# A Conformer block on eight cores: GLU blocks transposed in order and read by the conv matmuls with a step, W_v in halves, the conv finish spread over the output tiles

## The chip, the cores and the metric

The kernel runs on all 8 cores of one Trainium2 chip (trn2), two dies of four cores. Each core computes one of the 8 batch items on its own; nothing is exchanged. The metric is the device time of the slowest core in microseconds (us), median of several executions. Executions fall in a fast and a slow state: in the slow one the cores of a die show a lower granted TensorE clock (0.94 to 0.95 on cores 0 to 3 and 0.99 on cores 4 to 7 in the changed kernel's slow run of 2925 us). Only fast runs are compared here. Engines are PE (TensorE matmul), PEld (its weight loads), DVE (VectorE), ACT (ScalarE), POOL (GpSimd) and the DMA queues issued from SP and POOL.

## The reference, cut to what matters

```python
h = rms_norm(x)                              # x: (8, 2048, 2048) float32
u = h @ w_in                                 # conv value | conv gate | q | k | v, 1024 columns each
g = c_val * sigmoid(c_gate)                  # GLU
y = causal depthwise conv of g, width 31     # per channel, over the sequence
y = silu(layer_norm(y + b_dw))               # LayerNorm over the 1024 channels
a = chunked attention(q, k, v)               # 8 heads, band of 9 chunks of 64
x = x + concat(rms_norm(y), rms_norm(a)) @ w_out
x = x + relu(rms_norm(x) @ w1)**2 @ w2       # the FFN
```

## The kernel before

A small scheduler in the kernel's own Python code records operations with their dependencies, simulates them with rough durations, and so fixes the order of each engine's instructions. On the chip each engine is given its list in that order. `SLACK` is an extra delay that this simulation adds before a matmul may use what another engine produced; it changes only the order.

The stages, in order of time: V projection for 16 tiles of 128 positions; attention with the query and key projections; gates and depthwise conv for 8 blocks of 128 channels; the "finish" of the conv branch (normalisation and swish, by quarters of the sequence) between W_out tiles; FFN.

The depthwise conv runs on PE. A gated block `G` (128 channels x 512 positions) is transposed in 32x32 blocks into `Gt`. Then for each of 32 places `i` in a block of 32 two matmuls with small block-diagonal weights are made. Their moving operand is a row of `Gt` over 64 blocks (32 in the last two channel blocks):

```python
    Gt = [sb(f"Gt{i}", [32, 66], BF16, ...) for i in range(2)]     # place i, then block
    # conv_gate(cc, qd):
        stt(G[:, :], th[:, :], 1.0, ps(1), ALU.add, ALU.mult)      # the GLU
        o_ = bass.AP(gt, 1 + 16 * qd, [[32 * 66, 128], [1, 16], [66, 32]])
        P.vtr(o_, G[:, :].rearrange("p (b i) -> p b i", i=32), slow=3.6)
    # conv_dw(cc, q0, nq, bank):   n = 16 * nq
        for ih in range(2):
            ...                                                    # POOL builds the weights `pad`
            for i in range(16):
                mm(o_, pad[:, i, 0, :], gt[:, 16 * ih + i, c0:c0 + n], True, False)
                mm(o_, pad[:, i, 1, :], gt[:, 16 * ih + i, c0 - 1:c0 - 1 + n], False, True)
```

So the transpose writes 2-byte elements 132 bytes apart, and the matmul reads contiguous columns.

The V projection takes W_v in quarters of 256 columns, each loaded in one piece; quarters 2 to 4 wait for certain x tiles:

```python
        for hf in range(4):
            for k in range(16):
                mm(ps(hf, 0, 256), hT[:, qd, k, ti * 128:(ti + 1) * 128], wv[:, hf, k, :], k == 0, k == 15)
            act(V[:, t, 2 * hf:2 * hf + 2, 0:128], ps(hf, 0, 256)..., AF.Identity)
    for j in (1, 2, 3):
        ld[j].deps.add(xo_[2 * j - 1].i)          # quarter j waits for x tile 2j-1
```

## Time and profile before

| | before |
|---|---|
| time, 3 fast runs | 2785.1 us median (2784.4 to 2786.53) |
| PE busy | 2707 of 2782 us (97%) |
| DVE, ACT busy | 34%, 30% |
| start of the last V matmul (median of cores) | 181.6 us |

The first fence holds lines of the profile's page for the kernel before: busy time by engine, and the chain of work that ended last as shares of the span.

```profile
PE 2707.2 (97%) x14445; PEld 1327.1 (48%) x14704; DVE 932.3 (34%) x1482; ACT 830.9 (30%) x1601; POOL 228.1 (8%) x365
...
PE 94%; DMA 2%; issue 2%; DVE 1%; ACT 1%; ACTq 0%; DVEq 0%; SPq 0%; POOLq 0%
```

The chain says that nearly all of the time is PE's (94%). So in this kernel time taken from another engine should be worth something only where PE waits for it, and time added on PE should be added to the whole.

The next view is busy time by stretches, on the slowest core (core 0). The columns are the stretch, its length, then busy us (and instructions) of each engine, the granted clock (1.00 is full), the DMA share and GB/s.

```profile
0.00:20.00 20.00, 9.71 (x27) 4.46 (x28) 5.35 (x12) 6.68 (x9) 2.11 (x8) 1.00 0.87 214
20.00:40.00 20.00, 9.60 (x79) 7.13 (x77) 10.24 (x10) 11.30 (x19) 0.72 (x2) 0.83 1.01 232
40.00:60.00 20.00, 8.95 (x70) 6.93 (x70) 7.05 (x8) 8.01 (x12) 0.53 (x1) 0.66 1.00 290
60.00:80.00 20.00, 15.11 (x120) 12.01 (x118) 5.24 (x6) 9.48 (x18) 0.00 (x0) 0.83 0.46 162
...
720.00:740.00 20.00, 17.28 (x111) 7.98 (x110) 19.89 (x24) 10.92 (x15) 7.83 (x8) 1.00 1.00 207
```

PE stands half idle at the start, with the DMA engines full. At 720 us it waits for 2.7 of 20 us, and DVE has no free time there (19.89 of 20).

Two lines of the timeline show the conv matmuls (start, length, engine, line, operation, output <- inputs, count): a run of 32 with 64 columns takes 1.13 us, one with 32 columns 0.96 us.

```profile
518.91 1.13 PE L159 MATMUL ps<-Gt_112,pad 128*128 128x64 bf16 x32
...
702.82 0.96 PE L159 MATMUL ps<-Gt_112,pad 128*128 128x32 bf16 x32
```

And the groups of instructions by form (busy us, mean ns of one, idle time before) for the DVE transposes: the strided write takes 2.46 us, a transpose of the same 128x512 out of PSUM 0.73.

```profile
L206 DVE STREAM_TRANSPOSE Gt_112<-G 128x512 bf16<-128x512 bf16 x16 | 39.3, 2458 | 1.5
L206 DVE STREAM_TRANSPOSE Gt_113<-G 128x512 bf16<-128x512 bf16 x16 | 39.3, 2456 | 1.5
L206 DVE STREAM_TRANSPOSE y<-ps 128x512 f32<-128x512 f32 x32 | 23.3, 727 | 8.8 <-PE ps L159 7.9
```

### The profile page before, as it was taken

The page shows a single profiled execution, that of the slowest core. Times are in us where ns is not written, and L with a number is a line of the kernel's source. Part 1 is how long each engine was busy: PE and PEld are TensorE (multiplying, and loading weights), DVE is VectorE, ACT ScalarE, POOL GpSimd, SP SyncE. Part 2 cuts the span into 40 slices and gives each one's busy share as a digit, 9 for nine tenths or more (in the row PEclk, how much of TensorE's full clock was granted, in tenths as well). Part 3 has the DMA queues.
Part 4 walks back from the last instruction along what each step waited for, and adds up shares of the span by engine and source line. Part 5 has one row for each costly group of instructions (what it writes and reads, how often), then busy time and mean ns, then how long its engine had stood idle before and what let it go on. Part 6 is the DMA issues. An engine that isn't in the chain of part 4 may idle for free.

```text
span 2782.1 us, 38484 instructions; the slowest of 8 cores (2778.2 to 2782.1 us)
## 1 busy us (share of the span) xinstructions
PE 2707.2 (97%) x14445; PEld 1327.1 (48%) x14704; DVE 932.3 (34%) x1482; ACT 830.9 (30%) x1601; POOL 228.1 (8%) x365
## 2 busy tenths in 40 slices
PE   4999999999989999999999999999999999999999
PEld 3875555444444544444444444444444444444444
DVE  3236665655787522022131130220311302202113
ACT  4428887311376431211202102112022021120120
POOL 0000000422500000000000000000000000000000
PEclk8999999999999999999999999999999999999999
DMA  9411110324655478454444444579544444444424
GB/s 243 103 31 36 34 28 11 61 46 76 122 152 167 152 155 177 77 76 76 76 76 76 76 76 76 76 151 196 123 76 76 76 76 76 76 78 76 77 43 137
DMA packets 112455, 256.86 MB, mean 92 GB/s; under 512 B 5393, under 2 KB 83217, under 8 KB 94609
## 3 DMA queue, kind: packets, MB, share of 16 engines
q0 software_dynamic: 92112, 167.82, 37.9%
q1 hardware_dynamic: 20162, 86.56, 9.3%
q8 instruction: 122, 2.00, 0.3%
q14 instruction: 59, 0.48, 0.1%
HBM read 388.60 MB, written 33.55 MB: 152 GB/s over the span
## 4 chain that ended last, share of the span: by engine, by line
PE 94%; DMA 2%; issue 2%; DVE 1%; ACT 1%; ACTq 0%; DVEq 0%; SPq 0%; POOLq 0%
PE ps L159 93%; DMA xa_71<-x 1%; PE ps L163 1%; DMA acc<-out 1%; DMA wc_105<-wcg 0%; DVE y L198 0%; DVE y L192 0%; DVE hb_77 L198 0%; DVE Gt_113 L206 0%; ACT L178 0%; ACT hb_77 L178 0%; DVE hb_78 L198 0%; DVE y L206 0%; DVE yb L203 0%; DVE h2b L198 0%
## 5 line engine op out<-in xcount | busy, mean ns | idle before, releaser
L192 DVE TENSOR_TENSOR acc<-acc,ps 128x512 f32<-128x512 f32 x512 | 351.8, 688 | 1413.3 <-PE ps L159 1401.9
L159 PE MATMUL ps<-yb,fT 128*128 128x512 bf16 x2699 | 596.4, 379 | 4.0 <-DVE acc L192 1.1
L159 PEld LDWEIGHTS ps<-yb,fT 128*128 128x128 bf16 x2752 | 269.1, 98 | 326.3 <-issue 2.1
L178 ACT ACTIVATE rl_134<-ps 128x512 f32<-128x512 f32 x128 | 76.4, 597 | 1102.5 <-PE ps L159 1101.0
L159 PE MATMUL ps<-w2s_138,fT 128*128 128x512 bf16 x1317 | 292.4, 379 | 1.4
L159 PE MATMUL ps<-hTb,yb 128*128 128x512 bf16 x1024 | 242.2, 379 | 0.0
L159 PE MATMUL ps<-yb 128*128 128x512 bf16 x992 | 237.6, 379 | 1.7
L159 PEld LDWEIGHTS ps<-w2s_138,fT 128*128 128x128 bf16 x1344 | 131.5, 98 | 158.6
L225 POOL DMA_DIRECT2D yb<-w x75 | 66.6, 888 | 1173.8 <-PE ps L159 1105.6
L159 PEld LDWEIGHTS ps<-yb 128*128 128x128 bf16 x1024 | 100.2, 98 | 120.8
L159 PEld LDWEIGHTS ps<-hTb,yb 128*128 128x128 bf16 x1024 | 100.2, 98 | 120.3
L178 ACT ACTIVATE rl_135<-ps 128x512 f32<-128x512 f32 x128 | 76.4, 597 | 271.1 <-PE ps L159 271.1
L159 PE MATMUL ps<-wv,hT 128*128 128x256 bf16 x1024 | 120.6, 281 | 5.4 <-DMA wv<-wv 4.0
L159 PE MATMUL ps<-hTb,w1s_136 128*128 128x512 bf16 x512 | 121.0, 379 | 0.0
L159 PE MATMUL ps<-hTb,w1s_137 128*128 128x512 bf16 x512 | 121.0, 379 | 0.0
L159 PE MATMUL ps<-wo,yT 128*128 128x512 bf16 x497 | 117.1, 383 | 3.9 <-ACT yT L178 2.2
L159 PE MATMUL ps<-yb,w1s_136 128*128 128x512 bf16 x480 | 119.3, 379 | 1.7
L159 PE MATMUL ps<-yb,w1s_137 128*128 128x512 bf16 x496 | 117.5, 379 | 0.8
L159 PE MATMUL ps<-hT,wc_105 128*128 128x512 bf16 x498 | 115.0, 381 | 3.4 <-DMA wc_105<-wcg 2.5
L159 PE MATMUL ps<-hT,wc_104 128*128 128x512 bf16 x496 | 117.4, 379 | 0.9
L159 PE MATMUL ps<-wo,yb 128*128 128x512 bf16 x496 | 113.4, 379 | 0.8
L159 PEld LDWEIGHTS ps<-wv,hT 128*128 128x128 bf16 x1024 | 102.6, 101 | 20.6 <-issue 6.3
(300 smaller groups left out, 2741.1 us busy)
## 6 DMA issues: line engine op xcount, KB each, us to landing
yb<-w POOLq DMA_DIRECT2D x75, 1024.0 KB, 10.2
w2s_138<-w POOLq DMA_DIRECT2D x21, 1024.0 KB, 9.5
w1s_136<-w POOLq DMA_DIRECT2D x16, 1024.0 KB, 9.3
w1s_137<-w POOLq DMA_DIRECT2D x16, 1024.0 KB, 9.4
acc<-out SPq DMA_DIRECT2D x16, 1024.0 KB, 11.8
out<-acc SPq DMA_DIRECT2D x64, 256.0 KB, 7.5
wo<-wo POOLq DMA_DIRECT2D x8, 1024.0 KB, 13.4
xs_127<-x SPq DMA_DIRECT2D x6, 1024.0 KB, 6.4
```

The lines of the kernel that those rows point to most:

```text
L159: self.op("pe", lambda e: e.matmul(out, lhsT=lhsT, rhs=rhs, start=start, stop=stop, skip_group_check=skip), [lhsT, rhs], [out], f * max(n ...
L163: self.op("pe", lambda e: e.transpose(out, in_, ident), [in_, ident], [out], 64.0)
L178: self.op("act", lambda e: e.activation(out=out, in_=in_, func=func, scale=scale, bias=bias, **kw), r, w, d).func = func
L192: self._ew(eng, lambda e: e.tensor_tensor(out=out, in0=in0, in1=in1, op=op), [in0, in1], [out], fast)
L225: o = self.op(eng, lambda e: e.dma_start(out=out, in_=in_), r, w, 900.0 if eng == "pool" else 350.0, dma=True, key=key, nbytes=nb)
```

## The change

Its intent is to make the DVE transposes dense, to get the V projection going before all of W_v has landed, and to remove PE waits between the conv finish and the W_out tiles. The diff, cut to its core (an added `lazy` delay of zero is left out):

```diff
-SLACK = 400.0
+SLACK = 700.0
-    Gt = [sb(f"Gt{i}", [32, 66], BF16, ...)]
+    Gt = [sb(f"Gt{i}", [65, 32], BF16, ...)]
-        o_ = bass.AP(gt, 1 + 16 * qd, [[32 * 66, 128], [1, 16], [66, 32]])
-        P.vtr(o_, G[:, :].rearrange("p (b i) -> p b i", i=32), slow=3.6)
+        P.vtr(gt[:, 1 + 16 * qd:17 + 16 * qd, :], G[:, :].rearrange("p (b i) -> p b i", i=32))
-                mm(o_, pad[:, i, 0, :], gt[:, 16 * ih + i, c0:c0 + n], True, False)
-                mm(o_, pad[:, i, 1, :], gt[:, 16 * ih + i, c0 - 1:c0 - 1 + n], False, True)
+                mm(o_, pad[:, i, 0, :], gt[:, c0:c0 + n, 16 * ih + i], True, False)
+                mm(o_, pad[:, i, 1, :], gt[:, c0 - 1:c0 - 1 + n, 16 * ih + i], False, True)
...
-    wv_d = dr("wv", [4, 128, 16, 256])
+    wv_d = dr("wv", [2, 128, 16, 512])
+    # half 0 in 4 chunks of 4 k-blocks; x tile 1 waits for chunk 0, x tiles 2-4 for chunk 2
+        xo_[t].deps.add(ld[0 if t == 1 else 2].i)
+    # half 1 in 4 chunks, all waiting for x tile 3
+        o_.deps.add(xo_[3].i)
-        for hf in range(4):
+        for hf in range(2):
+            b = 2 * hf + t % 2
...
-    seq = [("c", 0), ("f", 1, 0, 4), ("a", 2), ("c", 1), ("f", 1, 4, 8), ("c", 2), ("s", 2), ("a", 3), ("c", 3), ("f", 2, 0, 3), ...
+    seq = [("c", 0), ("f", 1, 0, 2), ("a", 2), ("c", 1), ("f", 1, 2, 5), ("c", 2), ("f", 1, 5, 8), ("a", 3), ("c", 3), ("s", 2), ...
```

In `seq`, "a" and "c" are the attention and conv halves of a W_out tile, "s" the statistics of a quarter and ("f", q, i, j) the finish of its channel blocks i to j-1.

The moving operand of a conv matmul now has its columns 32 elements, 64 bytes, apart.

## The prediction

The forecast's sum came to -11 us, 2774 us in all. Its +11 us, for the conv matmuls that read with a step, was the author's estimate.

> **What bounds it now.** TensorE. The page's busy table gives PE 2707 of 2782 us, and the chain of waits is 94% PE. The timeline and the busy time by stretches show four stages:
> - 0-182 us, V projection. Its PE work is 16 tiles x (64 matmuls of 256 columns, 7.15 us, plus 16 transposes, about 0.9 us), about 129 us; so about 53 us are lost, all before 75 us. There the DMA engines are 87-101% busy to 60 us, an x tile (1 MB) takes about 4.4 us, PE waits for x and W_v, and the granted clock falls to 0.66-0.83.
> - 182-480, attention: PE 99% busy.
> - 480-980, conv, finish, W_out: PE 99% busy except 3 us at 660-672 (a gate weight load) and about 14 us at 720-820, where it waits for ScalarE and VectorE; VectorE is busy 19.9 of 20 us at 720-740.
> - 980-2776, FFN: matmuls back to back. Not touched.
>
> **What the change does.**
> 1. GLU transposes: 32 strided-output transposes of 2.456 us become dense. The PSUM-to-y transposes of the same 128x512 take 0.727 us, so I expect about 0.7 us: 56 us of VectorE saved. Nearly all is off the critical path; only those at 717-735 delay the first finish: 3 us gained.
> 2. Conv matmuls read their moving operand with a 64-byte step. Now 32 matmuls of 64 columns take 1.13 us, about 30 ns apart; 32 columns about 25 ns. [...]
> 3. W_v in 512-column halves: steady PE time is the same. Work on half 0 can start once 4 MB of W_v and x0 are in (about 25 us), and then each x tile (4.4 us of DMA) brings about 4.4 us of work while half 1 loads. PE should be mostly busy from about 28 us instead of 75 us, at 70-80% until half 1 has landed (about 65 us). V stage ends at about 168 instead of 182: 14 us gained (5 to 22).
> 4. Even finish: the waits at 784-803 (about 6 us on ScalarE results) mostly go: 5 us gained.
> 5. The larger scheduling slack only reorders; the added lazy term is zero. No effect that I can size.
>
> Sum: -14 + 11 - 3 - 5 = -11 us. **Predicted 2774 us**, 80% range 2758 to 2799. Faster by over 2%: 1%; within 2%: 98%; slower by over 2%: 1%.
>
> **What would show it.** First query/key projection matmul (182.4 us now) about 14 us earlier; PE busy at 20-60 us well above 18.5 of 40, its clock nearer 1. [...] GLU transposes about 0.7 us. VectorE busy down by about 55 us. PE idle at 720-820 about 6 us instead of 14. FFN unchanged at about 1797 us.
>
> **What would make it wrong.** The stride costing nothing (about 2763) or four times (about 2800). The start: PE runs a fixed order, so if half 1's matmuls stand ahead of ready half-0 work, chained loads leave it idle and the 14 us shrink or vanish.

## The result and the profile after

The three fast runs of the changed kernel take 2803.05 us in the median (2802.5 to 2805.2), those of the kernel before 2785.1. Each kernel had one slow run besides (2925 and 2999 us); with it the medians are 2804.12 and 2785.82. The ratio of fast runs is 1.0065, 95% interval 1.0043 to 1.0088. It is slower by about 18 us. Ratios here are the mean time of one kernel's fast runs over that of the other's of the same rounds, so they are not quite the ratio of the medians quoted.

Where the time went can be read from the first and last matmuls of each stage on each of the 8 cores (medians):

| stage | before | after | difference |
|---|---|---|---|
| start to the first gate matmul (V, attention) | 467.7 | 451.5 | -16.3 |
| first gate matmul to first W_out matmul | 262.9 | 302.3 | +39.4 |
| first W_out matmul to first W1 matmul | 302.2 | 297.1 | -5.1 |
| first W1 matmul to the end of the last matmul (FFN) | 1740.6 | 1740.6 | 0 |

Page line of the changed kernel: DVE is 53 us less busy, as forecast, and PE 40 us more.

```profile
PE 2747.7 (98%) x13917; PEld 1314.9 (47%) x14192; DVE 879.0 (31%) x1482; ACT 835.0 (30%) x1577; POOL 229.4 (8%) x369
```

The start, by stretches, again on the slowest core (core 4). PE is much busier at 40 to 60 us (17.00 instead of 8.95). At 20 to 40 us it still waits, and its clock is at half for nearly all of that time (0.51).

```profile
0.00:20.00 20.00, 12.02 (x32) 4.78 (x32) 5.35 (x12) 5.78 (x8) 3.36 (x10) 1.00 0.84 154
20.00:40.00 20.00, 7.92 (x30) 3.39 (x32) 3.17 (x3) 5.28 (x7) 2.12 (x4) 0.51 0.92 291
40.00:60.00 20.00, 17.00 (x108) 8.57 (x109) 14.11 (x13) 14.01 (x24) 0.00 (x0) 0.98 1.02 220
60.00:80.00 20.00, 16.12 (x87) 8.35 (x87) 3.82 (x4) 9.78 (x15) 0.00 (x0) 0.83 0.57 179
```

The transposes, by form: 0.71 us, as forecast.

```profile
L207 DVE STREAM_TRANSPOSE Gt_113<-G 128x512 bf16<-128x512 bf16 x16 | 11.4, 711 | 1.6
L207 DVE STREAM_TRANSPOSE Gt_112<-G 128x512 bf16<-128x512 bf16 x16 | 11.3, 709 | 1.3
```

The timeline of PE around the first conv block, and one run of 32 columns:

```profile
502.55 3.70 PE L160 MATMUL ps<-Gt_112,pad 128*128 128x64 bf16 x32
506.08 5.79 PE L160 MATMUL ps<-hT,wc_105 128*128 128x512 bf16 x25
511.70 3.70 PE L160 MATMUL ps<-Gt_112,pad 128*128 128x64 bf16 x32
515.23 1.00 PE L160 MATMUL ps<-hT,wc_105 128*128 128x512 bf16 x2
516.45 3.45 PE L160 MATMUL ps<-hT,wc_105 128*128 128x512 bf16 x10 [0.22 <-issue]
...
716.93 2.00 PE L160 MATMUL ps<-Gt_112,pad 128*128 128x32 bf16 x32
```

A run of 64 columns takes 3.70 us instead of 1.13, one of 32 columns 2.00 instead of 0.96; from start to start it is 110 and 57 ns per matmul instead of about 30 and 25. There are 12 of the first and 8 of the second: 12 x 2.57 + 8 x 1.04 = 39.1 us of added PE time, where I had forecast 11.

Look also at the gate matmuls (`hT,wc`) after each run. After the first, 25 of them take 5.79 us, the usual pitch of about 0.22 us. After the second, twelve stand in the 4.7 us from 515.23 to 519.90: about twice the usual spacing for most of that time (0.427 us from start to start; 0.216 is usual). There the clock was halved. The stretches show it; first the kernel before (500 to 700 us), then the changed one:

```profile
500.00:550.00 50.00, 48.86 (x335) 23.80 (x341) 27.55 (x32) 12.56 (x25) 26.59 (x26) 1.00 0.50 81
550.00:600.00 50.00, 49.71 (x277) 22.22 (x279) 28.89 (x26) 7.94 (x13) 11.94 (x13) 1.00 0.21 37
600.00:650.00 50.00, 49.47 (x326) 22.89 (x332) 31.92 (x29) 9.14 (x14) 19.25 (x19) 1.00 0.37 64
650.00:700.00 50.00, 47.02 (x287) 22.13 (x291) 25.31 (x21) 6.36 (x10) 13.99 (x16) 0.97 0.47 82
```

```profile
500.00:550.00 50.00, 49.51 (x276) 28.88 (x281) 16.75 (x24) 7.83 (x12) 20.43 (x21) 0.97 0.32 57
550.00:600.00 50.00, 49.56 (x246) 25.04 (x250) 14.77 (x21) 7.11 (x12) 9.88 (x10) 0.97 0.18 33
600.00:650.00 50.00, 49.73 (x265) 27.36 (x269) 13.20 (x18) 6.05 (x10) 13.12 (x14) 0.97 0.30 53
650.00:700.00 50.00, 49.08 (x253) 26.33 (x256) 19.40 (x26) 7.29 (x11) 16.54 (x17) 0.93 0.24 43
```

The clock column (third from the right) is where to look: 0.97 of 50 us is one stretch of 3.4 us at half clock, 0.93 is two. The clock record of the trace has 4 to 6 such stretches of 3.413 us between 495 and 700 us on each core of the changed kernel, 38 in all, and every one begins within 1 us of the end of a run of 32 strided matmuls. The kernel before has at most one, at 672 us, where PE waits for a gate weight load. And PE's busy column stays at 99%: on a busy engine this loss cannot be seen in the busy time.

### The profile page after: what moved, and what is told of

It reads as the page before. It is cut to its first block, busy times and chain, and to the rows that moved or that the text cites. A ratio compares the mean times of both kernels' runs of the same rounds, so it can differ in the third digit from the quotient of the medians.

```text
span 2803.6 us, 37361 instructions; the slowest of 8 cores (2795.3 to 2803.6 us)
## 1 busy us (share of the span) xinstructions
PE 2747.7 (98%) x13917; PEld 1314.9 (47%) x14192; DVE 879.0 (31%) x1482; ACT 835.0 (30%) x1577; POOL 229.4 (8%) x369
## 3 DMA queue, kind: packets, MB, share of 16 engines
q8 instruction: 117, 1.92, 0.3%
## 4 chain that ended last, share of the span: by engine, by line
PE 95%; DMA 2%; issue 1%; ACT 1%; DVE 1%; POOL 0%; SPq 0%; ACTq 0%; DVEq 0%; POOLq 0%
PE ps L160 94%; DMA wv<-wv 2%; PE ps L164 1%; DMA xa_74<-x 1%; ACT L179 0%; DVE y L199 0%; POOL pad L190 0%; POOL wv L226 0%; DVE y L193 0%; DVE yb L204 0%; ACT yb L179 0%; ACT h2b L179 0%; ACT y L179 0%; ACT yT L179 0%; ACT rs L179 0%
## 5 line engine op out<-in xcount | busy, mean ns | idle before, releaser
L160 PE MATMUL ps<-wv,hT 128*128 128x512 bf16 x497 | 117.6, 392 | 15.5 <-DMA wv<-wv 14.2
L160 PE MATMUL ps<-hT,wc_105 128*128 128x512 bf16 x499 | 120.6, 393 | 1.3 <-issue 0.7
L160 PE MATMUL ps<-hT,wc_104 128*128 128x512 bf16 x493 | 118.5, 383 | 0.8
L160 PE MATMUL ps<-hT,wqk_66 128*128 128x512 bf16 x374 | 95.9, 379 | 0.6
```

Source lines behind the costliest of these rows:

```text
L160: self.op("pe", lambda e: e.matmul(out, lhsT=lhsT, rhs=rhs, start=start, stop=stop, skip_group_check=skip), [lhsT, rhs], [out], f * max(n ...
```

## The experiments

Theory A: the strided moving operand makes the conv matmuls slower on PE itself, and the long runs of 32 slow matmuls also pull the clock down. Theory B: the new order (slack, finish) makes PE wait. "Before" in the tables is the kernel before, run in the same rounds on the same chip; times are medians of the fast runs. All kernels gave right results except sweep.

### Parts undone and parts alone

`dense` is the changed kernel with the old block layout:

```diff
-    Gt = [... [65, 32] ...]      # conv reads with a step of 32 elements
+    Gt = [... [32, 66] ...]      # conv reads contiguous columns, transposes write with a step
```

> The changed kernel with part 1 and 2 undone: the gated blocks are transposed with a step again, and the conv matmuls read 64 (or 32) contiguous columns; W_v halves, finish order and slack stay as changed. Theory A (the strided moving read costs PE time and drops the clock): runs of 32 conv matmuls of 64 columns back at 1.13 us (3.70 in the changed kernel), of 32 columns at 0.96 (2.00), no half-clock windows between 490 and 700 us, and the whole at about 2804 - 39 - 8 = 2757 us, so about 1% faster than the kernel before. Theory B (the loss comes from the new order: slack 700 and the finish spread): still about 2790 to 2804 us.

`before_stride` is the opposite, the kernel before with only the new block layout.

> The kernel before with part 1 and 2 of the change alone: dense block transposes, conv matmuls read with a 64-byte step. Theory A: about 2785 + 39 + 8 - 3 = 2829 us, conv runs of 3.70 us, several 3.4 us half-clock windows between 510 and 720 us. Theory B: 2785 us or less, since 56 us of VectorE work go.

`before_wv` is the kernel before with only the W_v part of the diff above.

> The kernel before with the W_v part alone (halves, chunks of 4 k-blocks, chained loads). From the stage ends of the changed kernel (first gate matmul 467 to 451 us, median of cores) theory A expects 16 us: 2769 us. If the start-up gain in the changed kernel came from the slack instead, about 2785.

| run | time | before, same rounds | ratio (95%) |
|---|---|---|---|
| dense | 2763.5 | 2784.1 | 0.992 (0.9892 to 0.9949) |
| before_stride | 2825.9 | 2784.1 | 1.0142 (1.0121 to 1.0163) |
| before_wv | 2762.7 | 2784.1 | 0.9917 (0.9897 to 0.9938) |

The layout costs 41.8 us alone and about 40 in the changed kernel (2803.1 - 2763.5). Theory B falls: without the layout the same order is faster than the kernel before. In dense the runs of 32 are back at 1.13 us, as this line of its timeline shows, and no core has a half-clock stretch between 455 and 700 us. Dense missed its expected 2757 by 6 us: that sum took 8 us for the clock and left out what the short transposes had gained.

```profile
503.32 1.13 PE L160 MATMUL ps<-Gt,pad 128*128 128x64 bf16 x32
```

W_v alone gives 21 us, more than the 16 expected. One thing did not fit: dense has W_v, the new finish order and the new slack, and is no faster than before_wv. That is taken up below.

### What the step costs: sweep, step4, step8

`sweep` reads the block buffer with a different step in each of the twelve runs of 64 columns:

```diff
+                sp = [1, 2, 3, 4, 5, 6, 8, 12, 16, 24, 31, 32][2 * cc + ih] if nq == 4 else 32
+                m_ = bass.AP(gt, i if nq == 4 else ..., [[2080, 128], [sp, n]])
```

The "line theory" of the next three records was a guess that no run had shown by then.

> Wrong result on purpose. The changed kernel; the twelve runs of 32 conv matmuls of 64 columns read the same block buffer with steps of 1, 2, 3, 4, 5, 6, 8, 12, 16, 24, 31 and 32 elements of 2 bytes, in that order of time. Line theory [...]: about 30 ns each up to step 4 (8 bytes), then a knee between 4 and 8, and from 8 (16 bytes) flat at about 110 ns whatever the step. Bank rival (large powers of two collide): 31 and 24 are much cheaper than 32 and 16. Plain-stride rival (any step but 1 is slow): step 2 is at 110 ns already.

`step4` and `step8` are right versions of the changed kernel, in which the buffer holds groups of g places (g = 4 and 8), so that a conv matmul reads with a step of g elements and the transpose writes runs of g elements:

```diff
-    Gt = [... [65, 32] ...]
+    Gt = [... [32 // g, 65, g] ...]
-        P.vtr(gt[:, 1 + 16 * qd:17 + 16 * qd, :], G[:, :].rearrange("p (b i) -> p b i", i=32))
+        o_ = bass.AP(gt, g * (1 + 16 * qd), [[2080, 128], [g, 16], [65 * g, 32 // g], [1, g]])
+        P.vtr(o_, G[:, :].rearrange("p (b a i) -> p b a i", a=32 // g, i=g))
```

> The changed kernel with the blocks stored in groups of four: the conv matmuls read with a step of 4 elements (8 bytes[...]), the block transposes write runs of 8 bytes. Line theory: conv runs of 32 take 1.13 us, no half-clock windows at 490 to 700, and the whole is as fast as the dense kernel (2764 us). Plain-stride rival: 3.7 us and about 2804 us. The block transposes should lie between 0.71 and 2.46 us; that changes the whole by under 3 us either way.

> The changed kernel with the blocks stored in groups of eight: a step of 16 bytes[...]. Line theory: as slow as the 64-byte step, 3.7 us for a run and 2804 us. Proportional rival (cost grows with the step): about a quarter of the loss, some 2775 us.

Sweep ran at 2793.7 us (one fast run; its time means nothing). Its timeline on core 0, the unbroken runs of 32 in order: steps 1, 2, 4, 5, 6, 8, 12, 16, 24, 31 and 32 (the run with step 3 was cut into pieces by other work; 29 of its 31 spacings can still be read):

```profile
492.80 1.12 PE L160 MATMUL ps<-Gt,pad 128*128 128x64 bf16 x32
499.36 1.17 PE L160 MATMUL ps<-Gt,pad 128*128 128x64 bf16 x32
...
518.81 2.11 PE L160 MATMUL ps<-Gt,pad 128*128 128x64 bf16 x32
545.76 2.55 PE L160 MATMUL ps<-Gt,pad 128*128 128x64 bf16 x32
553.76 2.98 PE L160 MATMUL ps<-Gt,pad 128*128 128x64 bf16 x32
581.58 3.87 PE L160 MATMUL ps<-Gt,pad 128*128 128x64 bf16 x32
590.90 3.87 PE L160 MATMUL ps<-Gt,pad 128*128 128x64 bf16 x32
619.61 3.93 PE L160 MATMUL ps<-Gt,pad 128*128 128x64 bf16 x32
630.67 3.80 PE L160 MATMUL ps<-Gt,pad 128*128 128x64 bf16 x32
663.09 3.71 PE L160 MATMUL ps<-Gt,pad 128*128 128x64 bf16 x32
671.60 3.69 PE L160 MATMUL ps<-Gt,pad 128*128 128x64 bf16 x32 [0.48 <-POOL pad L190]
```

From the starts of the matmuls in the trace, per matmul of 64 columns (a "line" is here 16 bytes of a partition, the step from which the spacing is flat; the lines touched are worked out from the step):

| step in elements (bytes) | ns from start to start | 16-byte lines touched | ns per line |
|---|---|---|---|
| 1 (2) | 29.8 | 8 | (does not show) |
| 2 (4) | 31.5 | 16 | (hardly shows) |
| 3 (6) | 46.0 | 24 | 1.92 |
| 4 (8) | 60.3 | 32 | 1.88 |
| 5 (10) | 74.1 | 40 | 1.85 |
| 6 (12) | 87.4 | 48 | 1.82 |
| 8 (16) | 115.3 | 64 | 1.80 |
| 12 to 16 | 115 to 117 | 64 | 1.80 to 1.83 |
| 24 to 32 | 110 to 113 | 64 | 1.71 to 1.77 |

The cost grows with the step up to 16 bytes and is flat after that. Steps of 31 and 24 are no cheaper than 32, so it is no collision of powers of two. Step 2 is nearly free, so it is not "any step but one" either. What fits all points is a charge of 1.7 to 1.9 ns for every 16 bytes touched, which does not show at steps 1 and 2 (29.8 and 31.5 ns), where such a line serves eight and four columns. This is an estimate from these spacings; no run looks inside the read. My line theory was right about the flat end from 16 bytes on, and wrong about the place of the knee: at step 3 the spacing is already 46 ns, and at step 4, where it still had about 30, it is 60.3, so the rate is half.

| run | time | before, same rounds |
|---|---|---|
| step4 | 2775.0 (ratio 0.9965, 0.9942 to 0.9988) | 2783.7 |
| step8 | 2808.5 (one fast run) | 2783.7 |

step4 missed its 2764 by 11 us; its runs of 64 columns take 2.10 us. The half rate costs 384 x 30 ns = 11.7 us, so the size fits, though not to the us: its three fast runs spread over 5.6 us. step8's runs take 3.88 us, and it is as slow as the 64-byte step.

### The clock by itself: interleave, interleave2

Here the strided matmuls stay, but later priorities set one or two dense gate matmuls between two of them:

```diff
+                if nq == 4:                  # interleave2: if nq == 4 and cc < 5:
+                    for e_ in (0, 1):
+                        P.ops[-1 - e_].prio = dw0 + 90 + 73 * ih + 1.5 * (2 * i + 1 - e_)
```

> The changed kernel, strided conv matmuls kept, but those of 64 columns are given later priorities, so that one to two dense gate matmuls stand between two of them. Theory A with the clock as a separate cost: each strided matmul still costs about 80 ns more than a dense one (30.8 us over 384), [...]the 4 to 6 half-clock windows at 490 to 700 us go and about 8 us come back: 2796 us. If the half-clock windows have another cause (waits, or fixed places in time), they stay and the time stays at 2804.

> As interleave, but the last of the six full conv blocks keeps its old priority, since in interleave a new wait of some 5 us stood at 697 to 707 us, where that block's late end held up the finish. In interleave the time from the 256th to the 640th gate matmul was 108.9 us without half-clock windows (changed kernel 112 with about two, dense 94.1). Clock as a separate cost: about 2804 - 6 = 2798 us. If the half-clock windows cost nothing, 2804 us.

interleave took 2805.4 us (three fast runs, ratio 1.0071, 1.0042 to 1.01), which missed the expected 2796: the late end of the last full block made a new wait just after 695 us. With that block left alone, interleave2 took 2797.9 (two fast runs, 2796.9 and 2798.9, where 2798 was expected). That is 5.2 us less than the changed kernel's 2803.05, or 3.7 less if each is taken against the kernel before in its own rounds: about 4 to 5 us. The stretches of interleave2 (its slowest core):

```profile
500.00:550.00 50.00, 50.00 (x282) 28.07 (x281) 12.76 (x19) 5.71 (x9) 13.95 (x15) 1.00 0.25 43
550.00:600.00 50.00, 50.00 (x266) 25.93 (x265) 19.64 (x28) 9.13 (x14) 15.00 (x15) 1.00 0.25 45
600.00:650.00 50.00, 50.00 (x273) 26.73 (x272) 13.80 (x19) 5.76 (x9) 13.95 (x14) 1.00 0.22 41
650.00:700.00 50.00, 48.87 (x259) 25.79 (x258) 18.63 (x25) 8.65 (x13) 16.10 (x17) 0.97 0.38 69
```

On all eight cores there is no half-clock stretch between 510 and 665 us, where the interleaved blocks run, and one at 669 to 685 us, at the one block left as it was. Cores 3 and 7 have one more, at 497 and 503 us. There the new priorities had left the very first run of 32 unbroken, and the stretch begins within 1 us of its end; on the other six cores the same run drew none. On the cores whose records are complete, the time over the first 640 gate matmuls is 161.1 us in dense, 179.3 in interleave2 (181 on cores 3 and 7), and 184 to 187 in the changed kernel. So some 18 us of that stage are the slow reads. The clock is 3.4 to 6.8 us more: by core, two to four stretches of 3.4 us at half speed. About 1 us of the difference is not accounted for. What is shown is that half-clock stretches began at the ends of unbroken runs of strided matmuls (all 38 in the changed kernel, after runs of 3.70 us), and that there were none where the runs were broken up. Why the clock falls there no run shows. In step4, whose runs take 2.1 us, no core has such a stretch between 505 and 700 us either; in sweep no core has one from 490 us on before the runs of 3.87 us begin, though those before it take up to 2.98.

### Finish order, slack and the W_v loads

`before_fin` is the kernel before with the new `seq` only; `before_slack` has `SLACK = 700.0` only; `wv_fin` is the W_v part and the new `seq` with the old slack (so dense with the slack back at 400).

> The kernel before with the new order of conv finish and W_out tiles alone (old slack, old transposes, old W_v). My prediction: 5 us faster, 2779. The dense kernel (W_v, order and slack: 2764) against before_wv (2763) says together nothing: then 2784, with the PE waits of 780 to 803 us gone but others come up at 720 to 760.

> The kernel before with the larger scheduling slack (700 instead of 400) alone. If the slack costs what the finish order gives: 2790 to 2795 us. If it only reorders, as predicted: 2784.

> The kernel before with the W_v part and the new finish order, but the old slack; dense (2764) with the slack back at 400. If the parts add up: 2763 - 9 = 2754 us, and the slack cost some 10 us in the changed kernel. If the finish order gains nothing once W_v is in halves: 2763.

| run | time | before, same rounds | difference |
|---|---|---|---|
| before_fin | 2774.7 | 2783.6 | -8.9 (ratio 0.9969, 0.9953 to 0.9984) |
| before_slack | 2791.8 | 2784.9 | +6.9 (ratio 1.0012, 0.998 to 1.0044) |
| wv_fin | 2754.2 | 2784.9 | -30.8 (ratio 0.9877, 0.9833 to 0.992) |

The ratios of the last two rows lean on one run of the kernel before that counts as fast at 2806.1 us; its six others lie at 2784.2 to 2785.3, and all five fast runs of before_slack at 2790.8 to 2792.7, so I take the 7 us as real although the interval holds 1. The stages agree: in before_slack the first gate matmul comes 3.5 us later than in the kernel before, and the stretch from the first W_out to the first W1 matmul is 4.2 us longer (306.4 against 302.2, medians of cores). In before_fin that stretch is 291.5. The lines for 780 to 800 us of the kernel before and of before_fin show the PE wait that went (15.20 and 20.00 us busy):

```profile
780.00:800.00 20.00, 15.20 (x113) 7.85 (x112) 12.53 (x21) 19.08 (x27) 0.00 (x0) 0.95 0.39 153
```

```profile
780.00:800.00 20.00, 20.00 (x128) 9.88 (x126) 17.14 (x27) 19.88 (x26) 0.00 (x0) 1.00 0.30 107
```

Finish order and slack cancel each other. For the finish order I had forecast 5 us and got 9; before_fin was expected at 2784, because I had read dense as "the finish order gives nothing", and that expectation missed. The larger slack, which I had put at zero, costs 7 us alone and 9 to 10 in the new order (dense 2763.5 against wv_fin 2754.2). The slack shifts waits to other places. Dense, then wv_fin, from 720 us (both on their slowest core):

```profile
720.00:740.00 20.00, 13.65 (x106) 6.28 (x104) 14.31 (x23) 12.43 (x20) 5.60 (x4) 0.74 0.47 100
...
780.00:800.00 20.00, 17.08 (x119) 8.82 (x117) 9.20 (x13) 18.00 (x23) 0.89 (x1) 0.97 0.59 171
```

```profile
720.00:740.00 20.00, 17.86 (x143) 8.47 (x141) 12.92 (x19) 10.34 (x16) 5.46 (x5) 0.74 0.37 77
...
780.00:800.00 20.00, 20.00 (x128) 9.95 (x127) 14.19 (x18) 14.92 (x22) 0.89 (x1) 1.00 0.69 186
```

PE is 4.2 and 2.9 us busier in these two stretches with the old slack. The larger slack also moves the last V matmul: 185 us in before_slack (median of cores), 181.6 in the kernel before.

`wv_nochain` is before_wv without the waits between x tiles and W_v chunks; `quarters_nochain` is the kernel before with its quarters, but without the waits that hold quarters 2 to 4 back:

> The kernel before with W_v in halves and the same eight chunk loads, but without the chain: x tiles 1 to 4 and the second half's chunks are issued at once. If the gain of 21 us comes from the order of the loads, x tiles and both halves now share the DMA engines from the start, the first half lands about twice as late and most of the gain is lost: 2775 to 2785. If it comes from the halves alone, 2763.

> The kernel before with its four W_v quarters, only without the waits that hold quarters 2 to 4 back behind x tiles. If the halves (half the work ready once 4 MB are in) make the gain: at most 5 us faster, 2779 to 2785. If the old waits were the cost: near 2765, as without the chain in halves.

wv_nochain took 2764.8 (before 2783.6, ratio 0.9932, 0.9917 to 0.9946): my expectation that the chain makes the gain missed. Its first half did not land twice as late either: the first 16 matmuls on it end at 30.6 us, in before_wv at 29.7. quarters_nochain took 2777.7 (before 2784.9, two fast runs, ratio 0.9962, 0.9905 to 1.0019), just outside the 2779 to 2785 expected; with two runs and an interval that holds 1 the split is rough. So of the 21 us about 7 seem to come already from not holding the quarters back, about 12 from the halves with their chunk loads, and 2 to 3 from the chain. Halves and chunks were not tested apart.

### A version that beats both: step2, wv_step2, wv_fin_step2

With groups of two, the conv reads with a step of 4 bytes, nearly free in the sweep (31.5 ns against 29.8), and the transpose writes runs of 4 bytes. `step2` is the changed kernel with g = 2, `wv_step2` the kernel before with the W_v part and g = 2, `wv_fin_step2` the same with the new finish order (old slack).

> The changed kernel with the blocks stored in pairs: the conv matmuls read with a step of 2 elements (4 bytes). The sweep had this at 31.5 ns for 64 columns, against 29.8 dense and 109.7 at 64 bytes; the block transposes should stay at 0.71 us as with groups of four. Theory (about 1.8 ns for each 16-byte line[...]): the conv stage is as the dense kernel's plus under 1 us, and the shorter transposes give about 5 us in the first finish, as step4 showed after its gates: about 2760 us, faster than both kernels. If the transposes are worth nothing: 2765.

> The kernel before with the W_v part and blocks in pairs, with its old finish order and slack. Against before_wv (2763 us) it shows what the short block transposes alone are worth: 3 us in my prediction, so about 2760. Against step2 it shows what the new finish order and slack are worth when the transposes are short: 5 us in my prediction, so step2 would be 5 us faster; nothing, if their gain moved to another wait.

> W_v part, new finish order, blocks in pairs (step of 4 bytes), old slack. If the parts add up: wv_fin less the 2 us that short transposes gave in wv_step2, about 2752; faster than step2 (2758), which has the larger slack. If the slack is innocent: 2758.

A line of step2 by form shows that runs of 4 bytes are enough for the fast transpose (0.71 us, as with runs of 8, 16 and 64 bytes in step4, step8 and the changed kernel; 2.46 us with 2-byte elements 132 bytes apart):

```profile
L207 DVE STREAM_TRANSPOSE Gt<-G 128x512 bf16<-128x512 bf16 x32 | 22.8, 711 | 5.3 <-PE ps L160 2.5
```

| run | time | before, same rounds | ratio (95%) |
|---|---|---|---|
| step2 | 2758.4 | 2783.6 | 0.991 (0.9889 to 0.9932) |
| wv_step2 | 2761.3 | 2783.6 | 0.9917 (0.9896 to 0.9938) |
| wv_fin_step2 | 2751.8 (two fast runs) | 2784.9 | 0.9869 (0.9813 to 0.9925) |

wv_fin_step2 is the fastest: 33 us below the kernel before and about 51 below the changed one. Short transposes alone are worth 1 to 2 us (wv_step2 against before_wv, within noise), 2.4 us in wv_fin_step2 against wv_fin, and about 5 in step2 against dense: they count only where DVE holds PE up.

## Why the prediction was wrong

It said 2774 us (2758 to 2799) and the time was 2803 to 2804. By terms, as the prediction put them (measured alone, medians of fast runs):

| term | predicted | measured |
|---|---|---|
| 1. short transposes | -3 | -1 to -5, by the version |
| 2. moving operand with a step | +11 (estimate without a measurement) | +39 on PE (run lengths), plus about 4 to 5 for the clock; +41.8 together with the transposes' gain |
| 3. W_v in halves | -14 | -21.4 |
| 4. even finish | -5 | -8.9 |
| 5. slack | 0 | +6.9 (9 to 10 in the new order) |

The measured parts add up: 41.8 - 21.4 - 8.9 + 6.9 = +18.4 us, and the two kernels differ by 18.0.

- **The step that failed** is step 2. That the loss falls on PE, fully on the critical path, was right. The size, +11 us, was an estimate that nothing measured backed: from start to start the matmuls take 110 ns with 64 columns and 57 with 32, where the kernel before has about 30 and 25. The prediction named a case of this size ("four times (about 2800)") but gave it too little weight. That its 2800 lies so near the 2803 measured is partly luck: the clock and the slack, which it left out, cost some 11 us, and W_v and the finish order gave some 11 us more than it said.
- **A term was missing.** After runs of 3.7 us of slow matmuls the granted clock was at half for windows of 3.4 us. The prediction had read the clock column at the start and did not ask it of the conv.
- **Slack** "only reorders; no effect that I can size": the order is what PE runs by, and it cost 7 us.
- **The gains were right in kind and too small**: W_v 21 for 14, finish 9 for 5. My fear that chained loads would make the gain shrink or vanish did not come true. In the changed kernel V ended at 167 us (median of cores), close to the 168 forecast, but this is luck in part: with the W_v part alone it ends at 163, and the larger slack alone puts it 4 us later. Details of step 3 were off all the same: at 20 to 40 us PE was busy for 7.9 us, far from "70-80%", and the clock there fell to 0.51; what made up for it came after 40 us.
- **Right:** transposes at 0.71 us, DVE less busy by 53 us (55 forecast), the FFN unchanged, and that almost none of DVE's time was on the critical path.

## What to carry to other kernels

Before moving a stride from one engine to another, ask which engine is the bound: here 56 us of DVE time off the critical path were bought with 39 us of PE time on it, and a layout between the two, in pairs of 4 bytes, served both engines at almost full speed (31.5 ns for a matmul of 64 columns against 29.8, 0.71 us for a transpose). When one operand's rate is in doubt by a factor of two to four, the range must hold both, and a sweep of the step in a single kernel run settles it. Test each part of a mixed change alone: here two good parts (30 us) hid behind one bad one, and a constant that "only reorders" took back most of one of them.
